# Latent attention with scores one block ahead and the value product one block later

## The chip, the cores and the metric

The kernel runs on one core of a Trainium2 chip. A core has five engines with instruction queues of their own: TensorE (PE; PEld is its weight load), VectorE (DVE), ScalarE (ACT), GpSimd (POOL) and SyncE (SP), which here issues all transfers. They share an on-chip memory (SBUF) and a small accumulator memory (PSUM, 8 banks of 2 KB per partition) and wait for one another through semaphores. The metric is the device time of one execution in microseconds (us).

## The reference

One layer of an encoder, 1024 tokens of width 1024, all in float32:

```
h = rmsnorm(x, norm_g);  proj = h @ w_in           # latents, conv, memory query, gates, r
q = rope(rmsnorm(rmsnorm(q_lat) @ w_uq))           # 8 heads of 96
k, v = from rmsnorm(kv_lat) @ w_ukv, k_pe          # 8 heads of 96 and of 64
s = q k^T * scale;  p = softmax(s);  o_attn = (p v) * silu(g_attn)
o_conv = B * conv3(C * u) * silu(g_conv)
o_mem = softmax(mq mk^T * scale) mv * silu(g_mem)  # 256 memory tokens, 4 heads
y = sum over branches of sigmoid(r_b + b_gate) * (o_b @ w_b)
return x + y @ w_out
```

## The kernel before

Every large matrix product is done as three products of float32r pieces: a value is split into a high piece (the rounded value) and a low piece (the rest), and high*high, high*low and low*high are added in PSUM. The layer runs in stages: norm and latents (`phase1`), then a long row of *feature matmuls* (`dense`, with bodies from `feat`, L526, L528, L530: 48 matmuls of 128x512 for each 128 columns of `w_in`), which go on beside everything else, memory attention (`mem_attn`), the latent attention (`mla`), and then the branch and output products (`phase3`).

The change is in `mla`. There are 8 heads and 8 blocks of 128 queries each, 64 blocks in all; the loop at its end runs over blocks `i` and emits, in each pass, pieces of several blocks. A generator, `self.pull(n)`, emits the next `n` feature matmuls, so that TensorE has work between the parts of attention; 744 of them are spread over the passes, and 72 are left for after the loop. The order in which TensorE, VectorE, ScalarE and GpSimd get their instructions is the order in which the code emits them (`manual_schedule`); that of SP's queue is set by a planner. Each engine works strictly in its order, and waits at an instruction until what it needs is there.

The parts of a block, or of a pair `u` of blocks (256 queries):

- `scores(i)`: six matmuls (L943) of a block's queries with all 1024 keys into a PSUM tile `s` (two banks; two such tiles).
- `exps(i)`: VectorE takes the row maximum `mx` from `s` (L948); ScalarE writes `p`, the exponentials, and their sum (L951). `p` has one buffer.
- `turn(i)`: VectorE copies `p` into two planes of 16 bits, `pl` (L85); SP issues a DMA transpose for each into `plt` (L86).
- `words(i)`: ScalarE joins the planes to transposed float32 words, `pw` (L90, two copies); GpSimd rounds them into the high piece `pth` (L969).
- `low(i)`: VectorE subtracts, `ptl` (L973).
- `pv(u)`: TensorE transposes the two blocks' reciprocal sums into the tile `po` (L984), and multiplies `pth`, then `ptl`, with the head's values into the same tile (L987, 8 matmuls each). `po` fills one bank, and has two buffers.
- `fin(u)`: ScalarE copies one half of the product, `otmp` (L1003); VectorE adds the halves and scales (L1004, L1005); in odd heads GpSimd multiplies with the gate and splits the result (L1010, L74, L80), and SP stores it.

A pass emits: the load of the next head's keys and values (in one of 8 passes), `exps(i)`, half of the pull, `low(i-4)`, `turn(i)`, `words(i-2)`, in odd passes `pv`, the rest of the pull, `scores(i+1)`, and in even passes `fin`. The feature matmuls have weights of their own, which GpSimd splits in parts of 256 columns (L74, L80), and their results are taken from PSUM by ScalarE (L620).

Of the kernel before, what the change touches and what calls it, by code (L numbers as in the profile page):

```python
# [9 lines left out]
F32 = mybir.dt.float32  # L10
F32R = mybir.dt.float32r
# [7 lines left out]
P = 128  # L19
S = 1024  # L20
D = 1024
TB = S // P
KT = D // P
M = 256
H = 8
DN, DR, DH, DV = 64, 32, 96, 64
# [4 lines left out]
NB = 256  # L31
# [31 lines left out]
class K:  # L63
# [563 lines left out]
    def phase2(self, st, sh):  # L627
        tc, nc, a, d = self.tc, self.nc, self.a, self.d
        v = nc.vector
        with ExitStack() as sm:  # L630
            mp = self.pool(sm, "mp", side="right")
            mt = M // P
            self.mk = [mp.tile([P, HM, M], F32R, name="mk" + x) for x in "hl"]
            self.mv = [mp.tile([P, mt, HM * DM], F32R, name="mv" + x) for x in "hl"]
            with ExitStack() as s2:
                self.ps = self.psum(s2, "ps1")
                self.nmm = 3
                self.mm = lambda hf: self.ps.tile([P, 512], F32, name="mm", bufs=self.nmm)
                with ExitStack() as s3:
                    wk = self.pool(s3, "wk1", side="right")  # L640
                    conv = self.conv_items(wk)
                    mkv = self.mkv_items(wk)
                    items = self.items
                    swq = self.st.enter_context(ExitStack())
                    wq = self.pool(swq, "wqm")
                    wq_t = [wq.tile([P, KT, 512], F32R, name="wq" + x) for x in "hl"]
                    for i, it in enumerate(conv):
                        if 3 < i <= 11:
                            it["eng"] = "AV"
                        items.append(it)  # L650
                        if 3 <= i < 11:
                            items.append(mkv[i - 3])
                        if i >= 12:
                            j = i - 12
                            dst = [t[:, 2 * j:2 * j + 2, :].rearrange("p a b -> p (a b)") for t in wq_t]
                            items.append(dict(src=a["w_qmem"][:, 2 * j:2 * j + 2, :].rearrange("p a b -> p (a b)"), dst=dst))
                    self.pull_to(440)
                    self.mem_norm(wk)
                    self.pull_to(1008)
                    self.mem_kv_a(wk)  # L660
                    self.pull_to(1056)
                    self.mem_kv_b(wk)
                    items += self.r_items()
                    items += self.br_items()
                    self.pull_to(1248)
            s_ps = st.enter_context(ExitStack())
            self.ps = self.psum(s_ps, "ps2")
            st.enter_context(tc.manual_schedule(engines={mybir.EngineType.PE}))
            self.mem_attn(sm, wq_t, swq)
            self.pull(-self.pulled % 24)  # L670
            s_ps.close()
        with ExitStack() as sm:
            self.ps = self.psum(st, "ps3")
            self.nmm = 2
            self.mla(sm, sh)

    def br_items(self):
# [219 lines left out]
        self.kvq = self.pool(self.s_kvq, "kvq", bufs=2)  # L897
        self.QB = {}

    def load_head(self, h):  # L900
        if h >= H:
            return
        nc, d, kp = self.nc, self.d, self.kvq
        k = kp.tile([DH, 2, S], F32R, name="k")
        vv = kp.tile([P, TB, 2 * DV], F32R, name="v")
        nc.sync.dma_start(k.bitcast(F32), d["k"][h])
        nc.sync.dma_start(vv.bitcast(F32), d["v"][:, :, h, :])
        self.HD[h] = (k, vv)

    def load_q(self, u):  # L910
        h, c = divmod(u, S // NB)
# [4 lines left out]
    def mla(self, st, sh):  # L916
        tc, nc, a, d = self.tc, self.nc, self.a, self.d
        v, ps = nc.vector, self.ps
        nj = NB // P
        NBLK = S // NB  # L920
        self.o = {}
        wk_s = st.enter_context(ExitStack())
        wk = self.pool(wk_s, "wk5", side="right")
        HD, load = self.HD, self.load_head
        SC, PL, PW, PT, MX, GA, PO, cur = {}, {}, {}, {}, {}, {}, {}, {}
# [6 lines left out]
        def scores(i):  # L932
            h, tb = divmod(i, TB)
            k = HD[h][0]
            if i % nj == 0:
                self.load_q(i // nj + 2)
            q = self.QB[i // nj]
            ts = slice(i % nj * P, (i % nj + 1) * P)
            s = SC[i] = ps.tile([P, S], F32, name="s", bufs=2)
            for qi, ki, s_, e_ in ((0, 0, True, False), (0, 1, False, False), (1, 0, False, True)):  # L940
                for hf in range(2):
                    c = slice(hf * 512, hf * 512 + 512)
                    nc.tensor.matmul(s[:, c], q[:, qi, ts], k[:, ki, c], start=s_, stop=e_)  # L943

        def exps(i):
            s = SC.pop(i)
            mx = MX[i] = wk.tile([P, 4], F32, name="mx", bufs=12)
            v.reduce_max(out=mx[:, 1:2], in_=s, axis=AX.X, negate=True)  # L948
            p = PL[i] = wk.tile([P, S], F32, name="p", bufs=1)

            nc.scalar.activation(out=p, in_=s, func=AF.Exp, bias=mx[:, 1:2], accum_out=mx[:, 2:3])  # L951
# [23 lines left out]
        def pv(u):  # L975
            h, blk = divmod(u, NBLK)
            vv = HD[h][1]
            pth, ptl = PT.pop(u)

            pb = PO[u] = ps.tile([P, 2, NB], F32, name="po", bufs=2)  # L980
            po, rb = pb[:, 0], pb[:, 1]
            for j in range(nj):
                r = MX.pop(u * nj + j)[:, 3:4]
                nc.tensor.transpose(rb[:, j * P:(j + 1) * P], r.broadcast_to([P, P]), self.ident)  # L984
            for t, s_, e_ in ((pth, True, False), (ptl, False, True)):
                for kb in range(TB):
                    nc.tensor.matmul(po, vv[:, kb, :], t[:, kb, :], start=s_ and kb == 0, stop=e_ and kb == TB - 1)  # L987
            if h % 2:
                GA[u] = wk.tile([P, NB], F32, name="ga")
                nc.sync.dma_start(GA[u], d["ga"][:, h // 2, blk * NB:(blk + 1) * NB])  # L990

        def fin(u):
            h, blk = divmod(u, NBLK)
            bs = slice(blk * NB, (blk + 1) * NB)
            pb = PO.pop(u)
            po, rb = pb[:, 0], pb[:, 1]
            pr, od = divmod(h, 2)
            if od == 0 and blk == 0:
                cur["o"] = wk.tile([P, S], F32, name="o", bufs=1)
            o = cur["o"]  # L1000
            a0, b0 = (0, 64) if od == 0 else (64, 0)
            tmp = wk.tile([P, NB], F32, name="otmp")
            nc.scalar.copy(tmp[a0:a0 + 64, :], po[b0:b0 + 64, :])  # L1003
            v.tensor_tensor(out=o[a0:a0 + 64, bs], in0=po[a0:a0 + 64, :], in1=tmp[a0:a0 + 64, :], op=ALU.add)  # L1004
            v.tensor_tensor(out=o[a0:a0 + 64, bs], in0=rb[a0:a0 + 64, :], in1=o[a0:a0 + 64, bs], op=ALU.mult)  # L1005
            if od == 1:
                gp = nc.gpsimd
                oh = wk.tile([P, NB], F32R, name="oah")
                ol = wk.tile([P, NB], F32R, name="oal")
                gp.tensor_tensor(out=o[:, bs], in0=o[:, bs], in1=GA.pop(u), op=ALU.mult)  # L1010
                self.split(o[:, bs], oh, ol)
                nc.sync.dma_start(d["oah"][:, pr, bs], oh.bitcast(F32))
                nc.sync.dma_start(d["oal"][:, pr, bs], ol.bitcast(F32))

        N = H * TB
        r_end = 1248 + 24 * 48
        rest = 72
        LAST = N + 4
        scores(0)
        for i in range(LAST + 1):  # L1020
            j = i + 1
            if i % TB == TB - 4 and 0 < i // TB < H:
                load(i // TB + 1)
            n = (r_end - rest - self.pulled) // (LAST + 1 - i)
            if i < N:
                exps(i)
            if i == 0:
                with tc.issue_after(self.turned):
                    load(1)
            self.pull(n // 2)  # L1030
            if 0 <= i - 4 < N:
                low(i - 4)
            if i < N:
                turn(i)
            if 0 <= i - 2 < N:
                words(i - 2)
            if i >= 5 and i % 2:
                pv((i - 5) // 2)
            self.pull(n - n // 2)
            if j < N:  # L1040
                scores(j)
            if i >= 6 and i % 2 == 0:
                fin((i - 6) // 2)
        man.close()
        self.parts = 1
        wk_s.close()
# [141 lines left out]
```

## Time and profile before

| | |
|---|---|
| device time, median of 3 runs | 1300.43 us (1297.37 to 1303.21) |
| the profiled execution: time, span | 1302.17 us, 1300.2 us |
| TensorE busy, mean granted clock | 1177.9 us (91%), 0.949 |
| VectorE, ScalarE, GpSimd busy | 691.6, 545.6, 519.3 us |
| first score matmul of `mla`, last start of a `ptl` matmul | 590.0 us, 1050.7 us |

Times in the profile's rows are counted from the start of the span. A busy TensorE is not one at its peak, since matmuls are pipelined and their ends are modelled: the distance between starts tells the pace. A granted clock of 1.00 is 2.4 GHz, one of 0.50 is 1.2 GHz. "Idle before, and its releaser" is the time for which an engine stood before an instruction, and whose work it waited for; a row that joins several instructions ends in xN.

### The profile page before, as it was taken

To read this page: it belongs to the slowest core of one execution; us is meant where nothing else is said; L and a number is where in the kernel's file an instruction comes from. 1 tells how busy PE (TensorE), PEld (TensorE's weight loads), DVE (VectorE), ACT (ScalarE), POOL (GpSimd) and SP (SyncE) were. 2 spreads that over 40 slices of the span, in tenths; PEclk is the share of its full clock that TensorE was granted. 3 is DMA by queue.
4 is the path that set the end of the run, shared out by engine and by line. 5 is a ranking of instruction groups with operands and counts; after the bars stand their busy time and mean duration, and the time that the engine had idled before them with its cause. 6 is when DMAs were issued, how large, how long until landed. Compare 5 with 4: busy or idle time off the path is not lost.

```text
span 1300.2 us, 15302 instructions
## 1 busy us (share of the span) xinstructions
PE 1177.9 (91%) x5458; PEld 989.6 (76%) x5458; DVE 691.6 (53%) x1084; ACT 545.6 (42%) x821; POOL 519.3 (40%) x478
## 2 busy tenths in 40 slices
PE   7999999999999998989887787788878898999998
PEld 7988777788888887777666676666666677888887
DVE  6987774433363365526556656555565511655421
ACT  6437665110120355545565666555565621322100
POOL 4456554332266333344334525423453452333300
PEclk8999999999999999999888989898899898999999
DMA  7438999422233344488656867565664469544431
GB/s 291 134 114 203 234 254 234 160 98 81 98 106 120 91 105 121 130 234 196 158 137 160 186 142 172 154 150 126 159 172 120 109 209 412 187 146 145 163 130 49
DMA packets 283821, 207.75 MB, mean 160 GB/s; under 512 B 201440, under 2 KB 253280, under 8 KB 282976
## 3 DMA queue, kind: packets, MB, share of 16 engines
q1 hardware_dynamic: 283744, 206.76, 57.4%
q8 instruction: 43, 0.70, 0.2%
q14 instruction: 34, 0.28, 0.1%
HBM read 108.14 MB, written 50.33 MB: 122 GB/s over the span
## 4 chain that ended last, share of the span: by engine, by line
PE 51%; DVE 13%; issue 11%; ACT 10%; DMA 7%; POOL 7%; SPq 1%; POOLq 0%; ACTq 0%; DVEq 0%
PE mm L530 7%; PE mm L526 7%; PE mm L528 6%; ACT pw L90 5%; DVE mx L948 4%; PE po L987 4%; PE mm L714 3%; PE mm L716 3%; PE mm L712 3%; PE s L943 3%; DVE ptl L973 3%; PE mm L109 2%; PE mm L111 2%; PE mm L110 2%; PE pq L293 2%
## 5 line engine op out<-in xcount | busy, mean ns | idle before, releaser
L526 PE MATMUL mm<-hh,whi 128*128 128x512 f32 x672 | 272.9, 406 | 3.5 <-DVE sg L603 3.5
L530 PE MATMUL mm<-hh,wlo 128*128 128x512 f32 x672 | 271.6, 406 | 0.8 <-POOL wlo L80 0.8
L528 PE MATMUL mm<-hl,whi 128*128 128x512 f32 x672 | 272.1, 405 | 0.0
L90 ACT COPY pw<-plt 128x1024 uint16<-128x1024 uint16 (+1 forms) x160 | 196.7, 1296 | 36.9 <-DMA plt<-pl 35.2
L969 POOL TENSOR_SCALAR pth<-pw 128x1024 fp32r<-128x1024 f32 x64 | 67.0, 1047 | 255.4 <-ACT pw L90 255.2
L74 POOL TENSOR_SCALAR whi<-wraw 128x256 fp32r<-128x256 f32 (+1 forms) x107 | 85.3, 797 | 209.1 <-PE pm L761 76.4
L80 POOL TENSOR_TENSOR wlo<-wraw,whi 128x256 fp32r<-128x256 f32 (+1 forms) x108 | 162.4, 1503 | 11.0 <-PE tr L318 1.5
L526 PEld LDWEIGHTS mm<-hh,whi 128*128 128x128 f32 x672 | 133.1, 198 | 31.8 <-DVE sg L603 4.4
L530 PEld LDWEIGHTS mm<-hh,wlo 128*128 128x128 f32 x672 | 133.2, 198 | 29.2 <-POOL wlo L80 1.3
L528 PEld LDWEIGHTS mm<-hl,whi 128*128 128x128 f32 x672 | 132.8, 198 | 27.6
L951 ACT ACTIVATE p<-s,mx 128x1024 f32<-128x1024 f32 x64 | 71.4, 1116 | 183.0 <-DVE mx L948 183.0
L987 PE MATMUL po<-ptl,v 128*128 128x256 f32 x256 | 55.5, 381 | 86.7 <-DVE ptl L973 86.7
L948 DVE TENSOR_REDUCE mx<-s 128x1 f32<-128x1024 f32 x64 | 78.0, 1218 | 105.0 <-PE s L943 104.5
L85 DVE COPY pl<-p 128x1024 uint16<-128x1024 uint16 x144 | 108.6, 796 | 21.1 <-ACT p L951 14.6
L987 PEld LDWEIGHTS po<-ptl,v 128*128 128x128 f32 x256 | 46.9, 270 | 93.2 <-DVE ptl L973 93.2
L943 PE MATMUL s<-k,q 96*128 96x512 f32 x384 | 104.1, 408 | 0.8 <-ACT sg L620 0.8
L943 PEld LDWEIGHTS s<-k,q 96*128 96x128 f32 x384 | 77.5, 202 | 19.9 <-ACT sg L620 1.2
L973 DVE TENSOR_TENSOR ptl<-pw,pth 128x1024 fp32r<-128x1024 f32 x64 | 81.8, 1279 | 0.5
L689 ACT ACTIVATE sg<-sg 128x1024 f32<-128x1024 f32 x24 | 25.4, 1061 | 85.2 <-DMA sg<-d_r 79.7
L620 ACT ACTIVATE sg<-mm,small 128x512 f32<-128x512 f32 x48 | 32.8, 685 | 56.4 <-PE mm L530 40.7
L391 ACT COPY pw<-plt 96x512 uint16<-96x512 uint16 x64 | 43.7, 773 | 27.5 <-DMA plt<-plq 18.8
L1004 DVE TENSOR_TENSOR o<-po,otmp 64x256 f32<-64x256 f32 x32 | 13.5, 422 | 64.5 <-ACT otmp L1003 59.3
(322 smaller groups left out, 2326.9 us busy)
## 6 DMA issues: line engine op xcount, KB each, us to landing
wraw<-in_w_feat SPq DMA_DIRECT2D x48, 512.0 KB, 3.7
d_r<-sg SPq DMA_DIRECT2D x24, 512.0 KB, 3.0
sg<-d_r SPq DMA_DIRECT2D x24, 512.0 KB, 4.2
d_k<-qkt SPq DMA_DIRECT2D x32, 192.0 KB, 3.1
d_q<-qkt SPq DMA_DIRECT2D x32, 192.0 KB, 2.9
q<-d_q SPq DMA_DIRECT2D x32, 192.0 KB, 2.9
k<-d_k SPq DMA_DIRECT2D x8, 768.0 KB, 6.8
wraw<-in_w_br SPq DMA_DIRECT2D x12, 512.0 KB, 4.2
```

The costliest lines, as they stand in the source:

```text
L74: nc.gpsimd.tensor_scalar(out=hi, in0=raw, scalar1=1.0, scalar2=1.0, op0=ALU.mult, op1=ALU.mult)
L80: e.tensor_tensor(out=lo, in0=raw, in1=hi.bitcast(F32), op=ALU.subtract)
L85: self.nc.vector.tensor_copy(pl[:, x], _halves(src, x))
L90: self.nc.scalar.copy(_halves(out, x), plt[:, x])
L526: mm(o, w1, self.hh[:, k, c], start=k == 0, stop=False)
L528: mm(o, w1, self.hl[:, k, c], start=False, stop=False)
L530: mm(o, w2, self.hh[:, k, c], start=False, stop=k == KT - 1)
L943: nc.tensor.matmul(s[:, c], q[:, qi, ts], k[:, ki, c], start=s_, stop=e_)
L948: v.reduce_max(out=mx[:, 1:2], in_=s, axis=AX.X, negate=True)
L951: nc.scalar.activation(out=p, in_=s, func=AF.Exp, bias=mx[:, 1:2], accum_out=mx[:, 2:3])
L973: v.tensor_tensor(out=lo, in0=PW.pop(i), in1=hi.bitcast(F32), op=ALU.subtract)
L987: nc.tensor.matmul(po, vv[:, kb, :], t[:, kb, :], start=s_ and kb == 0, stop=e_ and kb == TB - 1)
```

## The change

Five edits, all for the stage `mla`. (1) In the loop, `scores(i+1)` moves from the end of a pass to its head, in front of `exps(i)`. (2) `pv(u)` moves from pass 2u+5 to pass 2u+6, and `fin(u)` from pass 2u+6 to 2u+7; the loop has one pass more (70). (3) ScalarE's copy leaves `fin` for a function of its own, `head(u)`, which is emitted after `exps` of the same pass and so in front of `words`. (4) The tile `po` has one buffer in place of two, and the tiles of the feature matmuls three (`nmm`) in place of two. (5) From head 2 on, a head's keys and values come in two parts each, in passes 1, 2 (keys) and 5, 6 (values) of 8, where each came in one piece in pass 4.

On TensorE, around the first value product of the stage, before (`s_...` are score tiles, `mm_...` feature matmuls; `s_5199` is the sixth block's tile):

```order
L943 MATMUL s_5199<-k_4771,q_5013 128x512 x6
L530 MATMUL mm_5196<-hh_89,wlo_5035 128x512
L526 MATMUL mm_5196<-hh_89,whi_5034 128x512
L528 MATMUL mm_5196<-hl_90,whi_5034 128x512
L530 MATMUL mm_5196<-hh_89,wlo_5035 128x512
L526 MATMUL mm_5196<-hh_89,whi_5034 128x512
L984 MATMUL po_5231<-ident_64,mx_5022 128x128
L984 MATMUL po_5231<-ident_64,mx_5059 128x128
L987 MATMUL po_5231<-pth_5115,v_4772 128x256 x8
L987 MATMUL po_5231<-ptl_5116,v_4772 128x256 x8
```

and with the change (`s_5247` is the eighth block's tile; lines are shifted by 9):

```order
L952 MATMUL s_5247<-k_4771,q_5059 128x512 x6
L526 MATMUL mm_5203<-hh_89,whi_5041 128x512
L528 MATMUL mm_5203<-hl_90,whi_5041 128x512
L530 MATMUL mm_5203<-hh_89,wlo_5042 128x512
L526 MATMUL mm_5203<-hh_89,whi_5041 128x512
L528 MATMUL mm_5203<-hl_90,whi_5041 128x512
L993 MATMUL po_5277<-ident_64,mx_5029 128x128
L993 MATMUL po_5277<-ident_64,mx_5068 128x128
L996 MATMUL po_5277<-pth_5122,v_4772 128x256 x8
L996 MATMUL po_5277<-ptl_5123,v_4772 128x256 x8
```

The rows between a score block and a product are the same; two more score blocks stand ahead of the product. From there on the row of a pair repeats in both: score block, 10 to 11 feature matmuls, score block, 5, product, 5 or 6.

On ScalarE, in the second head, before (`p` are exponentials, `pw` words, `sg` the evacuation of a feature tile):

```order
L951 ACTIVATE p_5410,mx_5408<-s_5397,mx_5408 128x1024
L90 COPY pw_5425<-plt_5325 128x1024 x2
L620 ACTIVATE sg_5314<-mm_5316,small_73 128x512
L951 ACTIVATE p_5471,mx_5469<-s_5462,mx_5469 128x1024
L90 COPY pw_5486<-plt_5379 128x1024 x2
L1003 COPY otmp_5506<-po_5429 64x256
L951 ACTIVATE p_5512,mx_5510<-s_5499,mx_5510 128x1024
L90 COPY pw_5529<-plt_5418 128x1024 x2
```

and with the change:

```order
L960 ACTIVATE p_5417,mx_5415<-s_5350,mx_5415 128x1024
L1004 COPY otmp_5419<-po_5380 64x256
L90 COPY pw_5434<-plt_5331 128x1024 x2
L620 ACTIVATE sg_5320<-mm_5322,small_73 128x512
L960 ACTIVATE p_5462,mx_5460<-s_5408,mx_5460 128x1024
L90 COPY pw_5477<-plt_5367 128x1024 x2
L960 ACTIVATE p_5520,mx_5518<-s_5453,mx_5518 128x1024
L1004 COPY otmp_5522<-po_5483 64x256
L90 COPY pw_5539<-plt_5427 128x1024 x2
```

The copy `otmp` stood behind the pass's two `pw` copies and stands in front of them now.

The diff:

```diff
--- before.py
+++ after.py
@@ -671,7 +671,6 @@
             s_ps.close()
         with ExitStack() as sm:
             self.ps = self.psum(st, "ps3")
-            self.nmm = 2
             self.mla(sm, sh)
 
     def br_items(self):
@@ -897,15 +896,25 @@
         self.kvq = self.pool(self.s_kvq, "kvq", bufs=2)
         self.QB = {}
 
-    def load_head(self, h):
+    def load_head(self, h, part=None):
+
         if h >= H:
             return
         nc, d, kp = self.nc, self.d, self.kvq
-        k = kp.tile([DH, 2, S], F32R, name="k")
-        vv = kp.tile([P, TB, 2 * DV], F32R, name="v")
-        nc.sync.dma_start(k.bitcast(F32), d["k"][h])
-        nc.sync.dma_start(vv.bitcast(F32), d["v"][:, :, h, :])
-        self.HD[h] = (k, vv)
+        if part in (None, 1):
+            self.HD[h] = [kp.tile([DH, 2, S], F32R, name="k")]
+        if part in (None, 5):
+            self.HD[h].append(kp.tile([P, TB, 2 * DV], F32R, name="v"))
+        if part is None:
+            k, vv = self.HD[h]
+            nc.sync.dma_start(k.bitcast(F32), d["k"][h])
+            nc.sync.dma_start(vv.bitcast(F32), d["v"][:, :, h, :])
+        elif part < 5:
+            x = part - 1
+            nc.sync.dma_start(self.HD[h][0][:, x, :].bitcast(F32), d["k"][h][:, x, :])
+        else:
+            c = slice((part - 5) * TB // 2, (part - 4) * TB // 2)
+            nc.sync.dma_start(self.HD[h][1][:, c, :].bitcast(F32), d["v"][:, c, h, :])
 
     def load_q(self, u):
         h, c = divmod(u, S // NB)
@@ -977,7 +986,7 @@
             vv = HD[h][1]
             pth, ptl = PT.pop(u)
 
-            pb = PO[u] = ps.tile([P, 2, NB], F32, name="po", bufs=2)
+            pb = PO[u] = ps.tile([P, 2, NB], F32, name="po")
             po, rb = pb[:, 0], pb[:, 1]
             for j in range(nj):
                 r = MX.pop(u * nj + j)[:, 3:4]
@@ -989,6 +998,11 @@
                 GA[u] = wk.tile([P, NB], F32, name="ga")
                 nc.sync.dma_start(GA[u], d["ga"][:, h // 2, blk * NB:(blk + 1) * NB])
 
+        def head(u):
+            a0, b0 = (0, 64) if u // NBLK % 2 == 0 else (64, 0)
+            tmp = cur["t"] = wk.tile([P, NB], F32, name="otmp")
+            nc.scalar.copy(tmp[a0:a0 + 64, :], PO[u][b0:b0 + 64, 0])
+
         def fin(u):
             h, blk = divmod(u, NBLK)
             bs = slice(blk * NB, (blk + 1) * NB)
@@ -997,10 +1011,8 @@
             pr, od = divmod(h, 2)
             if od == 0 and blk == 0:
                 cur["o"] = wk.tile([P, S], F32, name="o", bufs=1)
-            o = cur["o"]
-            a0, b0 = (0, 64) if od == 0 else (64, 0)
-            tmp = wk.tile([P, NB], F32, name="otmp")
-            nc.scalar.copy(tmp[a0:a0 + 64, :], po[b0:b0 + 64, :])
+            o, tmp = cur["o"], cur["t"]
+            a0 = 64 * od
             v.tensor_tensor(out=o[a0:a0 + 64, bs], in0=po[a0:a0 + 64, :], in1=tmp[a0:a0 + 64, :], op=ALU.add)
             v.tensor_tensor(out=o[a0:a0 + 64, bs], in0=rb[a0:a0 + 64, :], in1=o[a0:a0 + 64, bs], op=ALU.mult)
             if od == 1:
@@ -1015,18 +1027,21 @@
         N = H * TB
         r_end = 1248 + 24 * 48
         rest = 72
-        LAST = N + 4
+        LAST = N + 5
         scores(0)
         for i in range(LAST + 1):
-            j = i + 1
-            if i % TB == TB - 4 and 0 < i // TB < H:
-                load(i // TB + 1)
+            if i > TB and i % TB in (1, 2, 5, 6):
+                load(i // TB + 1, i % TB)
             n = (r_end - rest - self.pulled) // (LAST + 1 - i)
+            if i + 1 < N:
+                scores(i + 1)
             if i < N:
                 exps(i)
             if i == 0:
                 with tc.issue_after(self.turned):
                     load(1)
+            if i >= 7 and i % 2:
+                head((i - 7) // 2)
             self.pull(n // 2)
             if 0 <= i - 4 < N:
                 low(i - 4)
@@ -1034,13 +1049,11 @@
                 turn(i)
             if 0 <= i - 2 < N:
                 words(i - 2)
-            if i >= 5 and i % 2:
-                pv((i - 5) // 2)
+            if i >= 7 and i % 2:
+                fin((i - 7) // 2)
+            if i >= 6 and i % 2 == 0:
+                pv((i - 6) // 2)
             self.pull(n - n // 2)
-            if j < N:
-                scores(j)
-            if i >= 6 and i % 2 == 0:
-                fin((i - 6) // 2)
         man.close()
         self.parts = 1
         wk_s.close()
```

## Rows read from the trace of the kernel before

**Rows 1.** Stage windows: us, busy us by engine, clock, DMA share, GB/s

```profile
590.00:611.00 21.00, 21.00 (x91) 17.16 (x92) 14.37 (x20) 12.38 (x16) 8.42 (x11) 1.00 0.78 179
611.00:1051.00 440.00, 353.27 (x1598) 295.03 (x1597) 264.50 (x364) 251.37 (x302) 184.04 (x221) 0.89 0.62 151
```

**Rows 2.** Waits in the same stretch: us, times, longest us

```profile
DVE mx L948 <- PE s L943: 104.5, 29, 5.3
PE po L987 <- DVE ptl L973: 86.7, 32, 3.7
DVE o L1004 <- ACT otmp L1003: 53.0, 28, 4.2
```

**Rows 3.** Timeline of one pair: start, length, engine, line, operation [idle before]

```profile
742.61 1.22 PE L987 MATMUL po<-ptl,v 128*128 128x256 f32 x8 [2.45 <-DVE ptl L973]
743.67 0.40 PE L526 MATMUL mm<-hh,whi 128*128 128x512 f32 x1
749.20 1.30 DVE L85 COPY pl<-p 128x1024 uint16<-128x1024 uint16 x2
751.52 0.38 PE L984 MATMUL po<-ident,mx 128*128 128x128 f32 x2
752.09 0.42 DVE L1004 TENSOR_TENSOR o<-po,otmp 64x256 f32<-64x256 f32 x1 [1.52 <-ACT otmp L1003]
754.01 1.21 DVE L973 TENSOR_TENSOR ptl<-pw,pth 128x1024 fp32r<-128x1024 f32 x1
755.27 1.75 PE L987 MATMUL po<-ptl,v 128*128 128x256 f32 x8 [2.42 <-DVE ptl L973]
```

**Rows 4.** Timeline, TensorE, first and late starts of the `ptl` half (32 in all)

```profile
614.73 1.28 PE L987 MATMUL po<-ptl,v 128*128 128x256 f32 x8 [2.34 <-DVE ptl L973]
...
642.65 1.76 PE L987 MATMUL po<-ptl,v 128*128 128x256 f32 x8 [2.63 <-DVE ptl L973]
...
1032.38 2.08 PE L987 MATMUL po<-ptl,v 128*128 128x256 f32 x8 [3.46 <-DVE ptl L973]
...
1049.76 1.22 PE L987 MATMUL po<-ptl,v 128*128 128x256 f32 x8 [0.60 <-DVE ptl L973]
```

**Rows 5.** Timeline of the opening: two `mx`, and the first product's transposes

```profile
599.39 1.20 DVE L948 TENSOR_REDUCE mx<-s 128x1 f32<-128x1024 f32 x1
...
603.22 1.21 DVE L948 TENSOR_REDUCE mx<-s 128x1 f32<-128x1024 f32 x1
...
611.07 0.38 PE L984 MATMUL po<-ident,mx 128*128 128x128 f32 x2
```

**Rows 6.** Timeline of VectorE beside GpSimd, and GpSimd alone

```profile
608.56 1.05 POOL L969 TENSOR_SCALAR pth<-pw 128x1024 fp32r<-128x1024 f32 x1 [0.44 <-ACT pw L90]
608.64 2.05 DVE L973 TENSOR_TENSOR ptl<-pw,pth 128x1024 fp32r<-128x1024 f32 x1
...
1048.48 1.23 DVE L973 TENSOR_TENSOR ptl<-pw,pth 128x1024 fp32r<-128x1024 f32 x1
1048.53 1.77 POOL L1010 TENSOR_TENSOR o<-o,ga 128x256 f32<-128x256 f32 x1 [1.03 <-DVE o L1005]
...
1050.87 0.74 POOL L80 TENSOR_TENSOR oal<-o,oah 128x256 fp32r<-128x256 f32 x1
1051.57 0.40 POOL L74 TENSOR_SCALAR whi<-wraw 128x256 fp32r<-128x256 f32 x1
```

**Rows 7.** Timeline, ScalarE: the last copy of `fin`

```profile
1055.62 0.36 ACT L1003 COPY otmp<-po 64x256 f32<-64x256 f32 x1
```

**Rows 8.** Waits of TensorE from 1051 to 1090 us

```profile
PE mm L712 <- DMA och<-d_och: 2.1, 2, 1.4
PE mm L714 <- DMA ocl<-d_ocl: 1.4, 3, 0.8
```

**Rows 9.** DMA, 611 to 1051 us: packets, MB, share of 16 engines

```profile
q1 hardware_dynamic: 149952, 65.96, 61.2%
```

**Rows 10.** Window of 10 us, columns as in rows 1

```profile
740.00:750.00 10.00, 7.55 (x38) 6.25 (x37) 7.24 (x10) 6.28 (x8) 3.31 (x6) 1.00 1.14 200
```

## The prediction

> **What bounds the kernel now.** I began with the stage windows: the latent-attention stage runs from the first scores at 590 us to the last value product at 1051 us, and in its main stretch TensorE is busy 353 of 440 us at a granted clock of 0.89, while VectorE (264), ScalarE (251) and GpSimd (184) are all further from full [rows 1]. No engine is full, so the stage is bound by waits. The table of waits names a ring of them: TensorE waits 86.7 us for `ptl` before the second half of the value product, VectorE 104.5 us for scores, and another 53.0 us in `fin` for the ScalarE copy of the product [rows 2].
>
> One pair of query blocks (two iterations) in the timeline shows the ring. TensorE starts the `ptl` half at 742.61, does 6 feature matmuls, one score block, 11 more, one score block, 5 more, the transposes and the `pth` half from 751.52 on, and then stands 2.42 us until `low` of VectorE, begun at 754.01, has ended [rows 3]. That `low` stands in the same iteration as the product that needs it, and behind a `mx` that needs a score block; the next score block stands behind the product. TensorE, VectorE and TensorE again, in series, once per pair.
>
> The price is 417.65 us from the first `ptl` half (614.73) to the one at 1032.38, 29 spacings: 14.40 us a pair [rows 4]. The work in a pair is less: 755.27 less 742.61 is 12.66 us, less the wait of 2.42 is 10.24 us at full clock, with 22 feature matmuls [rows 3]. Where the wait was 2.63 us, the next eight matmuls took 1.76 us in place of 1.22 [rows 3, 4]: the granted clock falls to its lower level, 1.2 GHz, for part of such a pair. The mean wait is 86.7 / 32 = 2.7 us; the other 1.5 of the 4.2 us between 10.2 and 14.4 are put down to the clock.
>
> **The change, part by part.** *Scores one block ahead, product one block later.* Per pair TensorE still does 12 score matmuls, the same feature matmuls and one product; only which score block stands ahead of which product changes: 8 blocks stand ahead of the first product, where 6 did. So `low` has a whole iteration before the product that reads it, and `mx` finds its scores ready. Both waits should go. Cost: the first product starts later. Before it there are 48 score and 65 feature matmuls where there were 36 and 55; the 91 took 21.1 us (590.0 to 611.07) [rows 1, 5], so the 113 take 26.2 us, and it starts at 616.2.
>
> TensorE's floor: 744 feature matmuls over 70 iterations are 21.3 a pair; 10.24 less 0.7 matmuls of 0.23 us is 10.1 us.
>
> What is late next is VectorE with GpSimd. VectorE's own round, with no product about, is 3.83 us an iteration (`mx` at 599.39 and 603.22) [rows 5]; with `fin`'s two operations of 0.42 us [rows 3] a pair is 8.5 us, under 10.1. But `low` (1.21 us) and the two plane copies (1.30 us) [rows 3] don't run beside GpSimd: a `low` that began 0.08 us after a `pth` took 2.05 us, and a gate multiply that began 0.05 us after a `low` took 1.77, where this kind of operation takes 0.74 alone [rows 6]. So I count them as one shared stretch. Per pair VectorE puts in 2 x (1.21 + 1.30) = 5.0 us; GpSimd two `pth` of 1.05, 1.9 parts of a weight split (62 parts over 32 pairs) of 0.40 + 0.74, so 4.3 us, and in every second head `fin`'s three operations, 0.74 + 0.40 + 0.74 = 1.9 more [rows 6]. Sums: 9.3 us in even heads, 11.2 in odd ones. Even heads are then TensorE's, odd heads the stretch's. I take 11.2 for the odd, and 10.4 for the even: 10.1 plus 0.3 for chance meetings, since 9.3 of 10.1 is nearly full. Mean 10.8 a pair. Bounds: 10.1 (everything meets gaps) and 12.0 (the second rival).
>
> *One bank for the product, three for features.* The next product must wait until `fin` has read the last one. `fin` stands a whole iteration ahead of it, so I cost it at nothing; the cover is that iteration, and what it costs without it is the last rival. The probability pieces have two buffers as before, so `pth` of a pair waits for the product two pairs back, now up to 2 us longer; the `low` that reads it is two iterations off. Nothing, unless GpSimd's queue is full; then the weight split behind it is late, with 22 matmuls (5 us) to spare.
>
> *Copy in front of the words.* The 0.36 us copy [rows 7] no longer stands behind `words`, so VectorE's 53.0 us of waits for it [rows 2] go. ScalarE may wait about 1 us for the product instead, with `words` behind it; ScalarE's pair is 251 us / 30.6 = 8.2 us of work [rows 1], so up to 1.9 us are free.
>
> *Keys and values in four parts.* Two more issues a head on SP's queue, the same bytes, earlier for the keys. Neither gain nor loss in the sum: the table of waits has no row for keys or values. It spreads 1.3 MB that now lands in two lumps among the plane transposes; between 0 and about 5 us of gain in all, I take 0.
>
> *The end.* The last `fin` copy now stands ahead of the feature matmuls' evacuations: it came at 1055.62, 4.6 us after the product's end [rows 4, 7]. The loads of the convolution branch queue behind `fin`'s stores, and TensorE later waits 3.5 us for them [rows 8]. Bounds 0 and 6 (with a slow clock after); I take 4.
>
> **Sum.** First product at 616.2; 28 pairs of 10.8 = 302.4; three products with no scores between them, each 22 feature matmuls of 0.23 and a product of 2.2 (two halves of 1.06, from 742.61 to 743.67 [rows 3], and the transposes), 7.3 each = 21.9; last product 2.2: end at 942.7, against 1049.76 + 1.22 = 1051.0 [rows 4]. That is 108.3 us, with the 4 of the end 112.3. The profiled execution took 1302.17 us, so 1189.9; the median of the runs shown is 1.7 us lower, so 1188 us.
>
> **Rivals.** *TensorE alone bounds*, 10.1 a pair: 28 x 0.7 = 20 us less, 1168. For it: VectorE's and ScalarE's own work fits. Against: the shared stretch of the odd heads is 11.2 by rows that show almost no overlap.
>
> *The shared stretch bounds everywhere.* GpSimd works in order and gets `pth` late from ScalarE, so its share can't be put where VectorE is in `mx`. If `low` and the copies wait for all of GpSimd's work and `mx`, the reciprocals and `fin` stand beside none of it, an odd pair is 11.2 plus half of the 3.6 us of those, 13.0, and an even one 11.1: mean 12.0, 28 x 1.2 = 34 more, 1222. Against: GpSimd was busy only 184 of 440 us [rows 1]. The Trainium skill, "SBUF — State Buffer", section "Who interferes with whom", states that VectorE and GpSimd share one port pair by an exclusive lock which whoever issues first holds for the whole instruction, while the other fully blocks, and that an operation with two SBUF inputs or in a two-port mode is affected. By that rule this rival stands, and a denser stage pays more of it; the 2.05 and 1.77 us agree with the rule.
>
> *The transfers bound.* The stretch moved 65.96 MB in 30.6 pairs, 2.16 MB a pair [rows 9]; a window of 10 us with a share over 1 had 200 GB/s [rows 10], at which 2.16 MB take 10.8 us. If that is the ceiling, the pairs with a key part (+0.46 MB on the mean) or a value part (+0.2) come out at 13.1 and 11.8, the others at 10.8: mean 11.6, 28 x 0.8 = 22 more, and with the slow clock back in a quarter of the pairs (28 x 1.5 / 4 = 10) 1220. For: 4 transposes a pair in one queue. Against: a block's words are taken up two iterations after its copies, 10.8 us here, and the opening's 3.83 us an iteration went through with 7.7 [rows 5].
>
> *Slower: the single bank.* If GpSimd's work holds `fin` back behind the plane copies, the next product waits for it in every pair, and the slow clock comes back with the waits (1.5 us a pair, as above). At 3.5 us of wait a pair is 10.1 + 3.5 + 1.5 = 15.1, the end at 616.2 + 423 + 24.1 = 1063, and the time 1308. It decides from 3.1 us per pair on, where a pair is 14.7. Against: `fin` would have to slip a full iteration.
>
> **Chances.** Forecast (1177 to 1203) 0.50; TensorE alone 0.15; shared stretch 0.18; transfers 0.11; slower 0.04, and 0.02 for something that eats all of it. Range 1166 to 1236: it takes in the two middle rivals and leaves out the tails. A measurement of this kernel can tell about 0.5%, 6.5 us; faster 0.94, same 0.02, slower 0.04.
>
> **What would show it.** Right: TensorE's wait for `ptl` under 10 us in all, `ptl` halves 10 to 11.3 us apart, further in odd heads, granted clock near 1.0 in the stage, VectorE no longer waiting for `otmp`, plane copies and `low` longer on the mean. Wrong: a new TensorE wait on `fin` before the transposes (single bank), ScalarE waiting on plane transposes (transfers), or spacings above 12 us in even heads.

## The result, and the profile after

The changed kernel takes 1172.13 us (median of 4 runs, 1169.31 to 1176.86), the kernel before in the same series 1298.9 (1295.94 to 1303.21): ratio 0.9025, 95% interval 0.8985 to 0.9066. The forecast was 1188 us, so the direction was right and the gain larger than forecast by 16 us: the time lies within the range given (1166 to 1236), and under the band of 1177 to 1203 that was given a chance of 0.50. The profiled execution took 1169.31 us, its span is 1167.6 us and its granted clock 0.993, where [rows 1] belong to one of 0.949.

The stage windows of the changed kernel, columns as in [rows 1]: opening, main stretch, last products, rest of the program.

```profile
590.00:613.50 23.50, 22.67 (x97) 17.76 (x96) 18.16 (x26) 17.22 (x22) 8.19 (x8) 1.00 0.81 180
613.50:896.00 282.50, 277.51 (x1440) 232.63 (x1439) 272.63 (x337) 233.47 (x278) 205.87 (x194) 1.00 0.97 216
896.00:930.00 34.00, 32.60 (x178) 27.87 (x177) 17.02 (x22) 17.87 (x21) 25.91 (x35) 1.00 0.52 140
930.00:1167.60 237.60, 232.27 (x1060) 193.05 (x1058) 87.07 (x118) 40.47 (x47) 57.53 (x32) 0.99 0.53 188
```

In the main stretch TensorE is busy 98% of the time, VectorE 96.5%, the DMA engines 97%, and the granted clock is 1.00 where it was 0.89 [rows 1]. An idle stage became a full one. The waits in the stage (590 to 930 us: us, times, longest us) say how; these are the rows that answer to [rows 2], and those that the change could have put in their place:

```profile
ACT p L960 <- DVE mx L957: 58.3, 55, 3.2
DVE ptl L982 <- POOL pth L978: 6.4, 3, 3.6
PE po L993 <- DVE o L1017: 5.5, 9, 1.4
ACT otmp L1004 <- PE po L996: 5.1, 2, 3.1
DVE pl L85 <- DMA plt<-pl: 3.4, 4, 1.7
DVE o L1016 <- ACT otmp L1004: 2.9, 1, 2.9
```

All three large rows of [rows 2] are gone: no wait of TensorE for `ptl` (86.7 before), none of VectorE for scores (104.5), and 2.9 us for `otmp` (53.0). ScalarE, 83% busy in the main stretch, now waits for VectorE's `mx`; that alone costs nothing, since it has room. TensorE's timeline: the stage's first scores, the first product (all three parts), the product 28 pairs later (its transposes), and the last one's `ptl` half:

```profile
586.21 3.06 PE L952 MATMUL s<-k,q 96*128 96x512 f32 x12 [0.78 <-ACT sg L620]
...
613.82 0.38 PE L993 MATMUL po<-ident,mx 128*128 128x128 f32 x2
613.95 1.20 PE L996 MATMUL po<-pth,v 128*128 128x256 f32 x8
614.99 1.12 PE L996 MATMUL po<-ptl,v 128*128 128x256 f32 x8
...
895.97 0.38 PE L993 MATMUL po<-ident,mx 128*128 128x128 f32 x2
...
920.25 1.12 PE L996 MATMUL po<-ptl,v 128*128 128x256 f32 x8
```

From 613.82 to 895.97 are 28 pairs of 10.08 us; before, 29 spacings of 14.40 [rows 4]. The brackets are empty from the transposes on: no wait. The stage's value products end at 921.4, against 1051.0. That is 129.6 us earlier; the rest of the span went from 249.2 us (1300.2 less 1051.0) to 246.2, another 3.0.

What fills VectorE is seen in a pair of an odd head (timeline, VectorE and GpSimd; start, length):

```profile
742.29 1.23 DVE L957 TENSOR_REDUCE mx<-s 128x1 f32<-128x1024 f32 x1
742.75 0.74 POOL L1022 TENSOR_TENSOR o<-o,ga 128x256 f32<-128x256 f32 x1
743.55 1.22 DVE L982 TENSOR_TENSOR ptl<-pw,pth 128x1024 fp32r<-128x1024 f32 x1
743.58 1.46 POOL L74 TENSOR_SCALAR oah<-o 128x256 fp32r<-128x256 f32 x1
744.88 1.85 DVE L85 COPY pl<-p 128x1024 uint16<-128x1024 uint16 x2
745.12 1.05 POOL L80 TENSOR_TENSOR oal<-o,oah 128x256 fp32r<-128x256 f32 x1
746.73 1.20 DVE L957 TENSOR_REDUCE mx<-s 128x1 f32<-128x1024 f32 x1
```

The gate multiply stands beside `mx` and takes 0.74 us, as it does alone. `oah` and `oal`, beside `low` and the copies, take 1.46 and 1.05 where 0.40 and 0.74 is their time alone [rows 6], and the copies 1.85 in place of 1.30 [rows 3]. The whole stage shows it by groups (busy us, mean ns of one, idle before), first before, 590 to 1051 us:

```profile
L85 DVE COPY pl<-p 128x1024 uint16<-128x1024 uint16 x128 | 93.9, 775 | 15.1 <-ACT p L951 14.6
L973 DVE TENSOR_TENSOR ptl<-pw,pth 128x1024 fp32r<-128x1024 f32 x64 | 81.8, 1279 | 0.5
L74 POOL TENSOR_SCALAR whi<-wraw 128x256 fp32r<-128x256 f32 x60 | 33.5, 558 | 1.3 <-PE mm L528 1.2
```

and after, 590 to 930 us:

```profile
L85 DVE COPY pl<-p 128x1024 uint16<-128x1024 uint16 x128 | 116.9, 953 | 14.0 <-ACT p L960 9.3 <-DMA plt<-pl 3.4
L982 DVE TENSOR_TENSOR ptl<-pw,pth 128x1024 fp32r<-128x1024 f32 x64 | 94.5, 1477 | 6.8 <-POOL pth L978 6.4
L74 POOL TENSOR_SCALAR whi<-wraw 128x256 fp32r<-128x256 f32 x61 | 54.9, 900 | 0.0
```

The same work meets more often in a denser stage: the means of these operations rise by 23, 15 and 61%. The transfers hold nobody up for long, though nearly all DMA engines are busy; the queue from 613 to 896 us, columns as in [rows 9]:

```profile
q1 hardware_dynamic: 142189, 60.69, 96.6%
```

The window's 216 GB/s are 43% more than the 151 of [rows 1], and VectorE waits 3.4 us for plane transposes in the whole stage. At the end of the stage the last `otmp` copy stands right behind the product (timeline, ScalarE), and TensorE waits 2.0 us for the branch's loads where it waited 3.5 [rows 8]:

```profile
921.41 0.36 ACT L1004 COPY otmp<-po 64x256 f32<-64x256 f32 x1 [3.11 <-PE po L996]
```
```profile
PE mm L713 <- DMA ocl<-d_ocl: 1.5, 2, 0.7
PE mm L711 <- DMA och<-d_och: 0.5, 1, 0.5
```

### The profile page after: what moved, and what is told of

It is laid out like the page before. It is cut to its first block, busy times and chain, and to the rows that moved or that the text cites. A ratio compares the mean times of both kernels' runs of the same rounds, so it can differ in the third digit from the quotient of the medians.

```text
span 1167.6 us, 15350 instructions
## 1 busy us (share of the span) xinstructions
PE 1125.0 (96%) x5458; PEld 945.8 (81%) x5458; DVE 721.0 (62%) x1084; ACT 549.3 (47%) x821; POOL 565.8 (48%) x478
## 4 chain that ended last, share of the span: by engine, by line
PE 41%; DVE 22%; DMA 13%; issue 11%; ACT 7%; POOL 4%; SPq 1%; ACTq 0%; DVEq 0%; POOLq 0%
DVE pl L85 8%; PE mm L526 5%; PE mm L530 5%; PE mm L528 5%; DVE mx L957 5%; DMA plt<-pl 5%; PE mm L713 4%; PE mm L715 4%; PE mm L711 4%; PE mm L109 3%; PE mm L110 3%; PE mm L111 3%; DVE ptl L982 2%; PE pm L760 2%; DMA plt<-plq 2%
## 5 line engine op out<-in xcount | busy, mean ns | idle before, releaser
L530 PE MATMUL mm<-hh,wlo 128*128 128x512 f32 x672 | 261.9, 392 | 1.2 <-POOL wlo L80 1.2
L528 PE MATMUL mm<-hl,whi 128*128 128x512 f32 x672 | 262.8, 391 | 0.0
L74 POOL TENSOR_SCALAR whi<-wraw 128x256 fp32r<-128x256 f32 (+1 forms) x107 | 107.2, 1002 | 199.5 <-PE pm L760 76.4
L80 POOL TENSOR_TENSOR wlo<-wraw,whi 128x256 fp32r<-128x256 f32 (+1 forms) x108 | 173.5, 1606 | 9.8 <-PE tr L318 1.6
L85 DVE COPY pl<-p 128x1024 uint16<-128x1024 uint16 x144 | 132.7, 961 | 20.0 <-ACT p L960 9.3
L978 POOL TENSOR_SCALAR pth<-pw 128x1024 fp32r<-128x1024 f32 x64 | 80.8, 1262 | 91.2 <-ACT pw L90 91.2
L982 DVE TENSOR_TENSOR ptl<-pw,pth 128x1024 fp32r<-128x1024 f32 x64 | 94.5, 1477 | 6.8 <-POOL pth L978 6.4
L718 DVE TENSOR_TENSOR acc<-mm,sg 128x512 f32<-128x512 f32 x16 | 10.9, 689 | 52.1 <-PE mm L715 40.3
L76 ACT CAST whi<-wraw 128x1024 fp32r<-128x1024 f32 x9 | 9.5, 1051 | 68.3 <-PE mm L528 66.8
L996 PE MATMUL po<-pth,v 128*128 128x256 f32 x256 | 38.4, 293 | 0.0
```

The lines of the kernel that those rows point to most:

```text
L74: nc.gpsimd.tensor_scalar(out=hi, in0=raw, scalar1=1.0, scalar2=1.0, op0=ALU.mult, op1=ALU.mult)
L80: e.tensor_tensor(out=lo, in0=raw, in1=hi.bitcast(F32), op=ALU.subtract)
L85: self.nc.vector.tensor_copy(pl[:, x], _halves(src, x))
L528: mm(o, w1, self.hl[:, k, c], start=False, stop=False)
L530: mm(o, w2, self.hh[:, k, c], start=False, stop=k == KT - 1)
L978: nc.gpsimd.tensor_scalar(out=parts(i)[0], in0=p, scalar1=1.0, scalar2=1.0, op0=ALU.mult, op1=ALU.mult)
```

## The experiments

"Pair" is the distance from the first `ptl` half to the 29th, divided by 28; the clock is that of 613 to 880 us. Ratios are to the kernel before on the same chip.

| run | median us | ratio, 95% interval | pair us | clock |
|---|---|---|---|---|
| e1 scores ahead only | 1201.86 | 0.9257 (0.9228 to 0.9285) | 11.01 | 0.98 |
| e2 product later only | 1189.77 | 0.9160 (0.9136 to 0.9185) | 10.63 | 1.00 |
| e3 changed kernel, copy behind the words | 1183.99 | 0.9116 (0.9097 to 0.9136) | 10.59 | 1.00 |
| e9 as e3, two product banks | 1185.38 | 0.9150 (0.9128 to 0.9173) | 10.53 | 1.00 |
| e4 changed kernel, keys and values whole | 1174.08 | 0.9040 (0.9017 to 0.9062) | 10.19 | 1.00 |
| e0 changed kernel again | 1172.39 | 0.9041 (0.9017 to 0.9065) | 10.10 | 1.00 |
| e5 changed kernel, two product banks | 1168.42 | 0.9011 (0.8983 to 0.9040) | 10.06 | 1.00 |
| e10 as e5, weight split in part on ScalarE | 1168.20 | 0.9007 (0.8987 to 0.9026) | 10.07 | 1.00 |
| e11 as e5, three plane buffers | 1171.50 | 0.9021 (0.8998 to 0.9043) | 10.06 | 1.00 |
| e6 216 fewer feature matmuls in the stage | 1213.94 | 0.9355 (0.9327 to 0.9382) | 9.96 | 1.00 |
| e7 as e6, without the gate's part (1 run) | 1201.88 | | 9.71 | 1.00 |
| e8 no feature matmuls in the stage (1 run) | 1313.99 | | 9.41 | 0.81 |

**Either move alone (e1, e2).** Each is one half of edits (1) and (2), put into the kernel before; the copy, the banks and the loads stay as they were (in e2 the load comes one pass later, so that it doesn't overwrite values in use, and the loop has one pass more).

```diff
 # e1
+            if i + 1 < N:
+                scores(i + 1)
             if i < N:
                 exps(i)
...
-            if j < N:
-                scores(j)
 # e2
-            if i >= 5 and i % 2:
-                pv((i - 5) // 2)
+            if i >= 6 and i % 2 == 0:
+                pv((i - 6) // 2)
...
-            if i >= 6 and i % 2 == 0:
-                fin((i - 6) // 2)
+            if i >= 7 and i % 2:
+                fin((i - 7) // 2)
```

> Of the change only the scores' move to the head of the pass; product, copy, banks and loads as before. Theory A (one block of slack cuts the ring): TensorE's wait for ptl falls from 86.7 us to under 15, a pair takes 10.5 to 11.2 us, since the copy of the product still stands behind the words and VectorE waits for it; about 1190 to 1205 us in all. Theory B (both moves are needed, each gives half): half of the wait stays, pairs near 12.2 us, 1225 to 1245 us.

> Of the change only the value product and fin one block later (and, because the values' buffer comes free later, the load of keys and values one pass later); scores, copy, banks as before. Theory A: as good as the scores' move alone within 10 us, 1190 to 1205 us, wait for ptl under 15 us. Theory B: half of the gain, 1225 to 1245 us. If VectorE still waits some 100 us for scores and the clock stays low, the scores' place was the cause and this run stays above 1250.

Waits from 613 to 880 us, e1:

```profile
DVE o L1004 <- ACT otmp L1003: 25.0, 22, 2.5
PE po L987 <- DVE ptl L973: 17.3, 20, 2.2
```

and e2:

```profile
DVE o L1004 <- ACT otmp L1003: 22.6, 22, 1.7
PE po L987 <- DVE ptl L973: 10.7, 13, 1.5
PE s L943 <- ACT p L951: 4.2, 10, 0.8
```

Each alone brings most of the gain: 7.4 and 8.4% of the 9.6 to 9.75% of all five edits. VectorE's wait for scores is in neither list, TensorE's for `ptl` is down to under 1 us a pair (in e1 17.3 us in all, a little over the 15 of theory A), and the clock is back to 0.98 and 1.00. e2 came out 0.2 us under the 1190 to 1205 of theory A, e1 within them. So the ring was in series, and one block of slack on either arc cuts it. That both were needed (theory B) is wrong. The sum of the two gains would be 15.8%; they are not additive, since each removes the same wait. How little the second cut adds is seen in e9 below, which has both moves and the copy behind the words: 0.9150, where e2 alone has 0.9160.

**The copy's place (e3, e9).** e3 is the changed kernel with the copy emitted in `fin`, behind the words; e9 gives it two product banks (and two feature banks) as well.

```diff
 # e3
-            if i >= 7 and i % 2:
-                head((i - 7) // 2)
             self.pull(n // 2)
...
             if i >= 7 and i % 2:
+                head((i - 7) // 2)
                 fin((i - 7) // 2)
 # e9, besides
-            pb = PO[u] = ps.tile([P, 2, NB], F32, name="po")
+            pb = PO[u] = ps.tile([P, 2, NB], F32, name="po", bufs=2)
```

> The changed kernel with the copy of the product put back behind the words. Theory A (VectorE is nearly full beside TensorE, so its waits count): VectorE waits about 1 us a pair for the copy, pairs near 10.9 us, 1190 to 1205 us, and TensorE waits for fin before the transposes, since there is one bank. Theory B (TensorE alone bounds, VectorE's waits are covered): 1172 us within 5.

> The changed kernel with the copy behind the words and two banks for product and features: only the two moves and the parts of keys and values. The run with the copy behind and one bank took 1184 us. Theory A (the copy's place costs by TensorE's wait for fin at the single bank, 15 us there): 1170 to 1174 us, as with the copy in front. Theory B (it costs by VectorE's own wait for the copy, 18.6 us there): 1179 to 1185 us.

Waits of e3, 613 to 880 us:

```profile
DVE o L1016 <- ACT otmp L1004: 18.6, 22, 1.7
PE po L993 <- DVE o L1017: 15.1, 21, 1.4
```

and of e9, where the second row is gone:

```profile
DVE o L1017 <- ACT otmp L1005: 18.7, 22, 1.7
PE s L953 <- ACT p L961: 7.4, 19, 0.8
```

Both waits stand in 21 or 22 of 25 pairs of e3. With two banks TensorE waits for `fin` no more, and the time is no better (0.9150 against 0.9116). So the copy's place costs through VectorE, which stands 0.85 us a time, and not through the bank, as theory B of e9 had it. With one bank it is worth 0.75% (0.9116 to 0.9041), some 10 us; with two it is 1.4% (0.9150 in e9, 0.9011 in e5), some 18 us. The expectation of e3 had the direction, with too large a price: 1184 us lies between its two theories.

**Keys and values whole (e4); two banks (e5).** e4 loads a head in one piece each in pass 5; e5 undoes edit (4), and e0 ran beside it.

```diff
 # e4
-            if i > TB and i % TB in (1, 2, 5, 6):
-                load(i // TB + 1, i % TB)
+            if i > TB and i % TB == 5:
+                load(i // TB + 1)
 # e5
+            self.nmm = 2
...
-            pb = PO[u] = ps.tile([P, 2, NB], F32, name="po")
+            pb = PO[u] = ps.tile([P, 2, NB], F32, name="po", bufs=2)
```

> The changed kernel with keys and values of a head in one piece each, in pass 5 of 8. Theory A (the parts do little): 1170 to 1180 us. Theory B (transfers are the second bound, 97% busy in the stage): the lumps hold the plane transposes back, TensorE waits once a head by 2 us or more, 1185 to 1200 us.

> The changed kernel with two banks for the product and two for the feature matmuls, as before the change. Theory A (the single bank costs): TensorE's waits for fin before the transposes (5.5 us, and some on the weight loads) go, 1164 to 1168 us. Theory B (they only move to another place, for instance to the evacuation of the feature matmuls, which has one bank less): 1171 to 1177 us.

> The changed kernel again, to set beside the run with two banks: 1172 us within 3.

In e4 VectorE waits 9.4 us for plane transposes from 613 to 880 us, in the changed kernel 3.4 (4.6 in e0), and three pairs take 11.4 to 11.8 us (one in e0, 11.6); the ratio is the same (0.9040, 0.9041), so edit (5) shortens these waits, and no time hangs on it that these runs can tell. In e5 TensorE's wait on `fin` is gone and the median is 4 us under e0's; the intervals overlap, so that edit (4) costs something is likely and not shown. e5 and e10 have the lowest medians of all.

**Is TensorE alone the bound? (e6, e8.)** The time came out where the rival "TensorE alone" put it. e6 takes 216 feature matmuls, some 6 a pair or 1.4 us of TensorE's work, out of the stage, e8 all 744 (`rest = 816`); they are done after the loop. If TensorE were the bound, pairs would fall to about 8.7 in e6. The edit of e6:

```diff
-        rest = 72
+        rest = 288
```

> The changed kernel with 288 in place of 72 feature matmuls kept for after the loop: 216 fewer in the stage, 6.2 a pair, 1.4 us of TensorE's work a pair, 49 us in all. Theory A (VectorE beside GpSimd is the next bound, close under TensorE): pairs fall only from 10.1 to about 9.5, TensorE waits again, 1200 to 1212 us; if the two engines never overlap, odd heads stay at 11 and even heads fall to 9.3. Theory B (TensorE alone bounds by far): pairs fall to 8.7 us and the whole stays at 1172 within 5.

> The changed kernel with all 744 feature matmuls of the stage put off until after it: TensorE has 5 us of work a pair, GpSimd no weight splits, ScalarE no evacuations, and 15 MB less are moved. Theory A (VectorE's round of 8.5 us is stretched by GpSimd's splits, about 0.8 us a pair): pairs of 8.6 to 9.0 us in even heads, 9.2 to 9.8 in odd ones. Theory B (VectorE and ScalarE bound by themselves): 9.5 to 10 in even heads as before. The whole gets longer by 744 x 0.23 = 170 us less 28 to 40 us, near 1310 us, which is not the point of the run.

Window and TensorE's waits of e6:

```profile
613.00:880.00 267.00, 235.48 (x1210) 188.40 (x1211) 258.44 (x322) 219.80 (x259) 172.19 (x156) 1.00 0.93 208
```
```profile
PE s L952 <- ACT p L960: 14.8, 22, 2.2
PE po L993 <- DVE o L1017: 14.6, 17, 1.3
PE po L993 <- ACT sg L620: 1.2, 1, 1.2
PE po L993 <- ACT pw L90: 0.9, 3, 0.5
```

and of e8:

```profile
613.00:880.00 267.00, 193.21 (x846) 153.67 (x845) 256.86 (x338) 219.44 (x256) 108.87 (x93) 0.81 0.80 179
```
```profile
PE s L952 <- ACT p L960: 57.2, 30, 5.1
PE po L993 <- ACT pw L90: 8.4, 7, 1.3
PE po L993 <- DVE o L1017: 7.6, 10, 1.1
```

In e6 a pair takes 9.96 us (10.39 in odd heads, 9.63 in even ones), 0.1 less than with all feature matmuls and more than the 9.5 of theory A: TensorE waits now, and VectorE is still busy 97%. So in the changed kernel, which has more weight splits than e6, VectorE's round with its collisions is at least about 10.0 us too, and the two are balanced. Without any feature matmul, and so without weight splits on GpSimd, VectorE is again at 96% and a pair takes 9.41: 9.62 in odd heads, where theory A gave 9.2 to 9.8, and 9.25 in even ones, where its 8.6 to 9.0 is missed. `low` takes 1.51 us on the mean there too (1.21 alone), beside `pth`. The 0.55 us a pair from e6 to e8 are an upper bound on what the splits left in e6 cost, since e8 also lacks the evacuations and the transfers of the feature matmuls.

**Whose collisions? (e7, e10.)** e7 is e6 without the gate multiply and its split on GpSimd in odd heads, and without the gate's load; the product without its gate is stored in place of the two pieces. e10 is e5 with the high piece of most weights taken by ScalarE.

```diff
 # e7
...
-                gp.tensor_tensor(out=o[:, bs], in0=o[:, bs], in1=GA.pop(u), op=ALU.mult)
-                self.split(o[:, bs], oh, ol)
...
 # e10
-                ... body=self.feat(fin)))
+                ... body=self.feat(fin), eng="AP" if f * 3 + b > 7 else "P"))
...
```

> The run with 288 matmuls kept back, and with GpSimd's three operations of fin in odd heads left out (the gate product and the split of latent attention; o is stored in their place, the gate's load is left out, the stores stay). In that run odd heads took about 0.8 us a pair more than even ones (10.4 against 9.6). Theory A (GpSimd's operations stretch VectorE's low and copies): odd heads fall to 9.5 to 9.7 as the even ones, about 1202 us. Theory B (the stores of the odd heads slow the transposes): odd heads stay above 10.2.

> The run with two banks (1168 us), and the high piece of the weights in the stage written by ScalarE in place of GpSimd: 0.4 us less for GpSimd per part, as much more for ScalarE. Theory A (GpSimd's operations stretch VectorE, which is 97% busy): VectorE gets shorter by some 10 us over the stage, TensorE's last waits go, 1162 to 1167 us. Theory B (ScalarE, 82% busy and in order, gives exponentials late): 1169 to 1180 us.

Odd heads of e7 take 9.91 us a pair (mean over three heads) where those of e6 take 10.39, even ones nearly the same (9.55 and 9.63): the gate's three operations, with its load, cost half a microsecond a pair in odd heads, not the 1.9 that the forecast added to its stretch. The 9.91 lies between the two theories of e7, nearer the first. In e10 GpSimd has 161 us of work from 613 to 880 us where e5 has 194, but VectorE is as full (257.9 against 257.3 of 267 us), its `low` and copies are no shorter (1.50 and 0.96 us on the mean against 1.49 and 0.97), and pair and time are those of e5. The time lies between the two theories. ScalarE did 14 us more in this stretch and that cost nothing either; with TensorE at 98.5%, little was left to win.

**The longer pairs (e11).** Nine of the 28 pairs of the changed kernel take 10.2 to 11.0 us, the others 9.5 to 10.1, ten of them 9.98. In eight of the nine TensorE stands before the product until VectorE is done with `fin` (0.15 to 0.89 us), in one before a score block (0.74 us): VectorE is late. In four of the nine VectorE has stood 0.55 to 1.65 us for a late plane transpose, as here in the chain of waits of the changed kernel (start, length):

```profile
820.26 6.39 DMA plt<-pl
826.73 1.90 DVE pl L85 x2
```

In the other five, all of odd heads, VectorE has no stop of over 0.25 us, and the operations that begin in such a pair keep it busy 10.0 to 10.9 us. e11 is e5 with a third buffer for the planes, and with two buffers for the words in place of three, to make room.

```diff
-            self.planes(p, wk.tile([P, 2, S], U16, name="pl", bufs=2), PL[i])
+            self.planes(p, wk.tile([P, 2, S], U16, name="pl", bufs=3), PL[i])
```

> The run with two banks (1168 us), and three buffers for the planes pl in place of two, so that a late plane transpose doesn't hold VectorE's copies; to have the room, two buffers for the words pw in place of three. Theory A (the longer pairs of 10.4 to 11 us come from late transposes, 4 to 6 us from issue to landing, that stop VectorE at the copies): VectorE's waits for transposes go, pairs stay within 10.2, 1162 to 1166 us. Theory B (transposes are late for want of transfer rate, so that the wait moves on to the words on ScalarE): 1167 to 1172 us, and ScalarE waits for transposes.

VectorE's wait for transposes is gone from 613 to 880 us, a wait for the words' buffer has come:

```profile
ACT pw L90 <- DVE ptl L983: 4.8, 12, 0.7
```

The longer pairs remain (10.2 to 11.0), and so does the time. Theory A, by which the plane buffer causes them all, falls: in none of e11's longer pairs does VectorE stop for over 0.25 us, and it is busy 261.5 of 267 us. What remains is VectorE's own work, lengthened beside GpSimd. How much the new wait for the words' buffer took back is not separated.

## Why the prediction was right, and where its size was off

- *A ring of waits bounds the stage.* Right: e1 and e2 cut it at different arcs, and both took away the same waits. The clock term (1.5 us a pair) was right as well: 14.40 less 2.7 of wait less 9.9 of work (98% of 10.08) leaves 1.8, and the granted clock went from 0.89 to 1.00.
- *First product at 616.2.* It came at 613.82. The stage's first scores came at 586.2, 3.8 us earlier than before, and from there it took 27.6 us, where 26.2 were put. The start is no effect of the change that can be told: the same kernel run again (e0) has its first `ptl` half at 619.53 instead of 614.99.
- *TensorE's floor of 10.1.* Too high by 0.3: where TensorE has no wait, pairs of 22 feature matmuls take 9.98 us, and those of 20, the first ten, 9.52, together 9.82 on the mean. The 10.24 was read from a pair with a wait, and counts the `pth` half up to its modelled end, 1.20 us; without a wait the `ptl` half starts 1.04 us after it (613.95 and 614.99 above).
- *What is late next is VectorE with GpSimd: one shared stretch, 11.2 us in odd heads, 10.4 in even.* This is the term that was mis-sized. VectorE is late next, as said: e6 shows its round at 10.0 us. But odd heads came out at 10.2 us a pair (even ones behind the first head at 10.1), and 11.2 us of work that never overlaps doesn't fit into 10.2. In the seven rows above, `low` and the copies (2.51 us alone) and `oah` and `oal` (1.14) would need 3.65 us in series; from 743.55 to 746.73 are 3.18. Over the main stretch VectorE was busy 272.63 / 28.02 pairs = 9.73 us a pair, where its own round is 8.5: it lost 1.2 us a pair to GpSimd's 4.3 to 6.2. GpSimd carried more, 205.87 / 28.02 = 7.35 busy, and had room.

  The Trainium skill, "SBUF — State Buffer", section "Who interferes with whom", has the second of two blocked for the whole instruction of the first, if the VectorE operation has two SBUF inputs or a two-port mode. The trace agrees but for a constant. `oah` behind a `low` took 1.46 in place of 0.40 us, while the gate multiply beside `mx`, which reads PSUM, kept its 0.74; but the `low` ended at 744.77 and `oah` at 745.04, which is 0.27 us later and not 0.40.

  So it is throughout. From 613.82 to 895.97 us the timeline has 236 meetings in which `low`, a plane copy or one of GpSimd's operations began over 0.15 us before the end of one on the other engine. In 232 of them it ended at the end of the first, plus its own time alone (`low` 1.21, one copy 0.69, `pth` 1.05, the others 0.40 or 0.74), less 0.13 to 0.15 us. In the other four, each of a `low` begun second, the GpSimd operation was the one that stood. The two meetings of [rows 6] show the same 0.13 and 0.15 us, so the forecast could have taken it off. In odd heads there were 9.3 such meetings a pair, worth 1.3 us: the 11.2 become 9.9 and fit into 10.2.
- *The sum.* 28 pairs at 10.8 less 10.08 are 20.2 us, the first product 2.4 earlier, and from 895.97 to 921.4 are 25.4 us where 24.1 were put for the last products, −1.3: together 21.3 us before the 942.7. The end gave 3.0 us where 4 were taken. In the profiled executions the gain was 132.9 us (1302.17 to 1169.31) against 112.3.
- *Copy in front of the words.* The 53.0 us of waits went, as said; with the ring cut they were worth some 10 us (e3) to 18 us (e9), since only 30.3 and 25.7 us of them were left in the stage without this edit.
- *Keys and values: 0.* Right within what can be told (e4).
- *Rivals.* The time is that of "TensorE alone" (1168), the cause is not: TensorE and VectorE have rounds of about the same length. That the rival's 10.1 a pair is also the 10.08 that was measured is luck: 9.82 is TensorE's pace, and the other 0.26 us are its waits for a late VectorE. "The shared stretch everywhere" (12.0) fell with the odd heads. "The transfers" fell: the ceiling of 200 GB/s was none, the stretch had 216 on the mean. "The single bank" has the wait that it named, 5.5 us in the stage and not 3.5 a pair; in e3, with the copy late, 20.0.

## What to carry to other kernels

When no engine is full and the same three waits come once per iteration, look for a ring, and cut it with one block of slack at the cheapest arc; a second cut at another arc adds little. What comes next is the fullest engine's own round: take it alone as one bound and with all collisions in series as the other (here 8.5 and 12.0, measured 9.7). To size a collision, compare in the rows at hand the end of the second operation with the end of the first plus the second's time alone; what they differ by (here 0.14 us) is to be taken off the sum once per meeting. To learn whether an engine that is 98% busy is the bound, take some of its work out: here the iteration hardly shortened, because another one was just as full.

## What the runs showed that was not expected

- Where VectorE and GpSimd collide, the operation that began second stands until the first has ended, and then needs 0.14 us less than alone (0.13 to 0.15 in 232 of 236 meetings). In the stage GpSimd's operations lengthened more (`whi` 0.40 alone, 0.90 on the mean) than VectorE's (copies 0.65 and 0.95).
- The DMA engines at a share of 0.97 over 282 us delivered 216 GB/s and made VectorE wait 3.4 us in the stage; a share near 1 was no sign of a bound.
- The granted clock stayed at 1.00 in e6, though TensorE stood 31.5 us in 43 short waits (longest 2.2 us) from 613 to 880 us; in e8, with 73.2 us in 47 waits of up to 5.1 us, it was 0.81. Before the change 86.7 us in 32 waits of up to 3.7 us went with 0.89 [rows 1, 2].
